# The low part of one weight load in four: a GpSimd-issued adding DMA in place of a VectorE subtraction

## The chip, the cores and the metric

One NeuronCore of a Trainium2 chip runs the whole program. The metric is the device time of one execution in microseconds (us).

In the text, TensorE (PE) multiplies matrices, VectorE (DVE) and ScalarE (ACT) work element by element, GpSimd (POOL) here only sets up constants, and SyncE (SP) issues the weight loads. A DMA transfer is issued by one of the engines' queues and carried out by 16 DMA engines that all queues share.

## The reference, cut to what matters

The reference is a two-layer encoder trunk on a sequence of 256 positions with 2048 features, in float32. Each layer normalises its input, multiplies it by a wide weight matrix, runs two token mixers (a bidirectional mLSTM and a bidirectional retention), and projects their outputs back:

```
h    = rmsnorm(x, norm_w)
proj = h @ w_in                                   # 2048 x 18448
q_m, k_m, v_m, z_m, o_m, g_m, q_r, k_r, v_r, z_r, gate_m, gate_r = split(proj)
...
y    = mix[:2048] * (u_m @ w_proj_m) + mix[2048:] * (u_r @ w_proj_r)
x    = x + y @ w_out                              # and a final rmsnorm
```

Nearly all of the work is in these products of a 256 x 2048 activation with 2048-row weights. What is computed of them does not change here, only how one operand is prepared.

## The kernel before

**Three multiplications for one.** TensorE is fed with a rounded format (`F32R`). So that the product stays accurate, each weight tile `raw` is split into a high part `whi` (the rounded weight) and a low part `wlo` (what the rounding lost), and so are the activations. `mm3` then adds three products into the same result: high by high, high activation by low weight, low activation by high weight.

**Blocks, loads and chunks.** The weights are worked off in blocks of 512 columns (the function `gemm`; eight of the 98 blocks, at the start of each layer, have 384 or 400 columns). The 2048 rows of a block come in four loads `i` = 0 to 3; each is one DMA from SyncE's queue into one of three `raw` buffers of 1 MB (128 partitions x 2048 elements). Each load makes two chunks (`half` = 0, 1; `KC` = 2, so 128 x 1024 elements each), so a block has the chunks 0 to 7, and the chunks 2 and 3 are those of load `i == 1`. A chunk is used by 12 matmuls (2 row groups of the weight, 2 halves of the sequence, 3 products).

**Who makes a chunk.** `wsplit` makes it: ScalarE writes `whi` as a rounded copy of `raw` (line 224), then VectorE writes `wlo` as `raw - whi` (line 225). There are three buffers of `whi` and three of `wlo`, so the parts of a chunk can be written when TensorE has done with the chunk three before it. A `raw` buffer can be loaded again when both of its chunks have been split. The last block of the program is done apart (tiles `wh` and `wl`).

**Order of the work.** Each engine has one queue that it works off in order. A scheduler sets the order; `tc.high_priority(offset=AHEAD)` lets the splitting and the loads of later chunks go ahead of the other work of ScalarE, VectorE and SyncE. Between chunks, `gemm` calls `run_later`, which puts in pieces of the attention work of earlier blocks, so that TensorE finds it between its blocks.

**Small row buffers.** The tag `row` holds 128 x 512 tiles: the mixing bias `bm`, the decay table `dec`, the last norm's weight `fw` and scratch of the first statistics `sq0`. `bm`, `dec` and `fw` are loaded from ScalarE's queue.

Of the kernel before, what the change touches and what calls it, by code (L numbers as in the profile page):

```python
# [9 lines left out]
F32 = mybir.dt.float32  # L10
F32R = mybir.dt.float32r
I32 = mybir.dt.int32
AF = mybir.ActivationFunctionType
ALU = mybir.AluOpType
AX = mybir.AxisListType

P = 128
# [5 lines left out]
NB = 512  # L23
# [6 lines left out]

# 512-column blocks of a layer's weights, in the order in which the host packs them
B_QK_M = 0
# [14 lines left out]
KC = 2  # L47
# [11 lines left out]
def encoder_kernel(ctx: ExitStack, tc: tile.TileContext, x, x_t, positions, w_main, w_qk0, w_qk1, b_mgate, vecs, b_mix,  # L59
                   final_norm_w, inv_freq, rpieces, decay, out):  # L60
    nc = tc.nc
# [3 lines left out]
    wp = ctx.enter_context(tc.tile_pool(name="wp", bufs=3))  # L65
    tmp = ctx.enter_context(tc.tile_pool(name="tmp", bufs=2))
# [7 lines left out]
    def t512(name, dtype=F32):  # L74
        return tmp.tile([P, 512], dtype, name=name, tag="t512", bufs=6)
# [3 lines left out]

# [1 line left out]
    x_sb = const.tile([P, NT, D], F32, name="x_sb")  # L81
# [36 lines left out]
    def late_setup():  # L118
# [28 lines left out]

        # adding and subtracting 1.5 * 2^(23 + b) rounds to a multiple of 2^b
        def drop_turns(v, magic):
# [22 lines left out]

# [1 line left out]
    def rsqrt_mean(dst, ss, n, count, base=EPS):  # L174
# [46 lines left out]

    def wsplit(raw, whi, wlo):
        with tc.high_priority(offset=AHEAD):
            nc.scalar.copy(out=whi, in_=raw)  # L224
            nc.vector.tensor_tensor(out=wlo, in0=raw, in1=whi.bitcast(F32), op=ALU.subtract)  # L225
# [24 lines left out]
    def gemm(xhi, xlo, src, name, n=NB, ahead=(), before=None):  # L250
        ps = [pg.tile([P, NB], F32, name=f"{name}{t}", tag="g")[:, 0:n] for t in range(NT)]
        for ck in range(NCK):
            if before is not None:
                before(ck)
            elif ck >= 3:
                run_later()
            i, half = divmod(ck, KD // KC)
            if half == 0:
                raw = ahead[i] if i < len(ahead) else wraw(src, i)
            whi = wp.tile([P, KC * NB], F32R, name="whi", tag="whi", bufs=3)[:, 0:KC * n]  # L260
            wlo = wp.tile([P, KC * NB], F32R, name="wlo", tag="wlo", bufs=3)[:, 0:KC * n]
            wsplit(raw[:, half * KC * n:(half + 1) * KC * n], whi, wlo)
            for k in range(KC):
                kt = ck * KC + k
                for t in range(NT):
                    mm3(ps[t], xhi, xlo, t, kt, whi[:, k * n:(k + 1) * n], wlo[:, k * n:(k + 1) * n],
                        kt == 0, kt == KT - 1)
        return ps
# [18 lines left out]
    def x_stat(c, ss, first=False):  # L287
        for t in range(NT):
            junk = tmp.tile([P, NB], F32, name="sq0", tag="row", bufs=4) if first else t512("sq")
            nc.scalar.activation(out=junk, in_=x_sb[:, t, c * NB:(c + 1) * NB], func=AF.Square,  # L290
                                 accum_out=ss[:, t * NBLK + c:t * NBLK + c + 1])
# [15 lines left out]
    def mlstm_gates(gates, gate_out):  # L307
        g4 = gates.rearrange("p t (d k h) -> p t d k h", d=2, k=2)

        # log-sigmoid, decays summed along the sequence in both directions  # L310
        def small(name):
# [30 lines left out]

        # stabilised gate weights
        wt = bigt("wt", 2)
# [141 lines left out]
    def ret_scores(h, qr_hi, qr_lo, st_out):  # L486
        dec = tmp.tile([P, NB], F32, name="dec", tag="row", bufs=4)
        nc.scalar.dma_start(out=dec[:, 0:3 * P], in_=decay[h])
# [31 lines left out]

# [1 line left out]
    ht_hi, ht_lo, ss_x = new_ht()  # L522
# [25 lines left out]
    for l in range(DEPTH):  # L548
        gate_out, hm_out = [], []

        # mLSTM queries and keys: convolution along the sequence, SiLU
        qk_hi, qk_lo = bigt("qkm_hi", 3, F32R), bigt("qkm_lo", 4, F32R)
# [37 lines left out]

        # mLSTM attention matrices, both directions joined
        at = bigt("at", 5, F32R)
# [12 lines left out]

        # retention: rotary queries and keys
        qr_hi, qr_lo = bigt("qkr_hi", 2, F32R), bigt("qkr_lo", 4, F32R)
# [33 lines left out]

        # mLSTM output gate and per-head statistics
        hm = hm_out[0]
# [16 lines left out]
        for b in range(NBLK):  # L660
            ps = gemm(ht_hi, ht_lo, wmain(l, B_Z_M + b), "zm")
            ev = []
            for t in range(NT):
                z = t512("z")
                nc.scalar.activation(out=z, in_=ps[t], func=AF.Silu, scale=rs[t])
                i = t * NH_M + b
# [7 lines left out]
        def branch(b_gate, u_hi, u_lo, b_proj, first):  # L674
            for b in range(NBLK):
                bm = tmp.tile([P, NB], F32, name="bm", tag="row", bufs=4)
                mc = (0 if first else D) + b * NB
# [40 lines left out]

        # output projection, residual
        if l < DEPTH - 1:  # L720
# [8 lines left out]

# [1 line left out]
    halves = NBLK + 1  # L731
# [22 lines left out]
    for b in range(NBLK):  # L754
        fw = tmp.tile([P, NB], F32, name="fw", tag="row", bufs=4)
        nc.scalar.dma_start(out=fw, in_=final_norm_w[b * NB:(b + 1) * NB].rearrange("(o n) -> o n", o=1)
# [41 lines left out]
def _pack(inputs):  # L798
    import numpy as np

    def chunks(w):
        # [2048, n] to [chunk, partition, (k n)]
        n = w.shape[1]
        return w.reshape(NLD, KD, P, n).transpose(0, 2, 1, 3).reshape(NLD, P, KD * n)
# [31 lines left out]
def _constants():  # L836
    import numpy as np
    freq = np.power(10000.0, -np.arange(64) / 64).astype(np.float32)[None, :]
    # 1 / (2 pi) in pieces of twelve significant bits
    digits = 0x28BE60DB9391054A7F09D5F47D4D3770  # L840
# [30 lines left out]
```

## Time and profile before

| what | value |
|---|---|
| time, median of 3 runs | 2237.16 us (2236.63 to 2237.55) |
| span of the profiled execution, first to last instruction | 2235.9 us |
| TensorE busy | 2218.1 us, 99% of the span |
| VectorE busy | 1331.9 us, 60% |
| ScalarE busy | 1086.0 us, 49% |
| GpSimd busy | 1.7 us, 0% |
| granted TensorE clock, mean | 0.999 of full speed |
| moved by DMA | 419.49 MB, 188 GB/s on average |

The profiled execution has no time of its own beside its span; the span is 1.3 us shorter than the median of the timed runs. Busy time counts the stretches in which an engine carries out at least one instruction. Matmuls overlap, so their single durations add up to more than the busy time of TensorE.

### The profile page before, as it was taken

How to read it: one execution, taken by the hardware profiler on the slowest of the kernel's cores; microseconds unless marked ns; L12 is line 12 of the kernel's file. 1: busy time of each engine (PE TensorE's matmuls, PEld its weight loads, DVE VectorE, ACT ScalarE, POOL GpSimd, SP SyncE). 2: the span in 40 equal slices, each digit the busy share in tenths (PEclk: the TensorE clock that was granted, in tenths of full speed). 3: DMA queues.
4: the chain of work that ended last, by engine and by line, in shares of the span. 5: the costliest groups of instructions: out<-in, count | busy, mean ns of one | idle time of the engine just before them, and what ended most of it. 6: DMA issues, size and time to landing. Idle time of an engine off the chain costs nothing.

```text
span 2235.9 us, 26069 instructions
## 1 busy us (share of the span) xinstructions
PE 2218.1 (99%) x10360; PEld 1868.6 (84%) x10360; DVE 1331.9 (60%) x1809; ACT 1086.0 (49%) x1380; POOL 1.7 (0%) x10
## 2 busy tenths in 40 slices
PE   8999999999999999999999999999999999999998
PEld 8888888888888888888898888888888888888887
DVE  6887665555555455555578746655555555555555
ACT  7654344555544454444457544445554434444444
POOL 0000000000000000000000000000000000000000
PEclk9999999999999999999999999999999999999999
DMA  7544455455555555555455445544555555555553
GB/s 281 189 156 167 175 190 186 177 190 188 189 196 197 203 187 189 196 190 195 171 169 195 153 166 188 195 167 182 198 186 191 203 193 196 186 195 191 199 190 148
DMA packets 66426, 419.49 MB, mean 188 GB/s; under 512 B 8192, under 2 KB 10496, under 8 KB 20224
## 3 DMA queue, kind: packets, MB, share of 16 engines
q1 hardware_dynamic: 61120, 409.44, 51.0%
q10 hardware_dynamic: 5184, 8.39, 1.1%
q8 instruction: 81, 1.33, 0.2%
q14 instruction: 41, 0.34, 0.0%
HBM read 415.70 MB, written 2.10 MB: 187 GB/s over the span
## 4 chain that ended last, share of the span: by engine, by line
PE 97%; DMA 1%; ACT 1%; DVE 0%; issue 0%; SPq 0%; ACTq 0%
PE gt L231 5%; PE gt L230 5%; PE pj L230 5%; PE gt L229 5%; PE pj L231 5%; PE pj L229 5%; PE vr L229 3%; PE wo L229 3%; PE wo L231 3%; PE vr L230 3%; PE vm L230 3%; PE vm L229 3%; PE wo L230 3%; PE zm L231 3%; PE om L229 3%; PE vr L231 3%
## 5 line engine op out<-in xcount | busy, mean ns | idle before, releaser
L225 DVE TENSOR_TENSOR wlo<-raw,whi 128x1024 fp32r<-128x1024 f32 (+2 forms) x776 | 933.0, 1203 | 818.0 <-ACT whi L224 816.6
L224 ACT CAST whi<-raw 128x1024 fp32r<-128x1024 f32 (+2 forms) x776 | 803.1, 1035 | 1007.1 <-PE gt L231 203.7
L229 PE MATMUL gt<-whi,ht_hi 128*128 128x512 f32 x512 | 200.1, 391 | 0.0
L231 PE MATMUL gt<-whi,ht_lo 128*128 128x512 f32 x512 | 199.3, 389 | 0.0
L230 PE MATMUL gt<-wlo,ht_hi 128*128 128x512 f32 x512 | 199.2, 389 | 0.0
L229 PE MATMUL qk<-whi,ht_hi 128*128 128x384 f32 (+2 forms) x320 | 112.3, 352 | 7.5 <-ACT whi L224 7.5
L230 PE MATMUL qk<-wlo,ht_hi 128*128 128x384 f32 (+2 forms) x320 | 112.5, 351 | 0.3 <-DVE wlo L225 0.3
L231 PEld LDWEIGHTS gt<-whi,ht_lo 128*128 128x128 f32 x512 | 96.1, 188 | 20.0
L230 PEld LDWEIGHTS gt<-wlo,ht_hi 128*128 128x128 f32 x512 | 96.2, 188 | 19.7
L229 PEld LDWEIGHTS gt<-whi,ht_hi 128*128 128x128 f32 x512 | 96.1, 188 | 19.7
L231 PE MATMUL qk<-whi,ht_lo 128*128 128x384 f32 (+2 forms) x320 | 111.9, 350 | 0.0
L229 PE MATMUL zm<-whi,ht_hi 128*128 128x512 f32 x256 | 100.2, 391 | 0.0
L229 PE MATMUL qr<-whi,ht_hi 128*128 128x512 f32 x256 | 100.2, 391 | 0.0
L229 PE MATMUL zr<-whi,ht_hi 128*128 128x512 f32 x256 | 100.2, 391 | 0.0
L229 PE MATMUL vr<-whi,ht_hi 128*128 128x512 f32 x256 | 100.1, 391 | 0.0
L230 PE MATMUL vr<-wlo,ht_hi 128*128 128x512 f32 x256 | 99.9, 390 | 0.0
L229 PE MATMUL vm<-whi,ht_hi 128*128 128x512 f32 x256 | 99.9, 390 | 0.0
L230 PE MATMUL vm<-wlo,ht_hi 128*128 128x512 f32 x256 | 99.7, 390 | 0.0
L231 PE MATMUL vm<-whi,ht_lo 128*128 128x512 f32 x256 | 99.7, 389 | 0.0
L231 PE MATMUL zm<-whi,ht_lo 128*128 128x512 f32 x256 | 99.7, 389 | 0.0
L231 PE MATMUL qr<-whi,ht_lo 128*128 128x512 f32 x256 | 99.7, 389 | 0.0
L231 PE MATMUL zr<-whi,ht_lo 128*128 128x512 f32 x256 | 99.7, 389 | 0.0
(255 smaller groups left out, 4205.7 us busy)
## 6 DMA issues: line engine op xcount, KB each, us to landing
raw<-in_w_main_dram SPq DMA_DIRECT2D x360, 1024.0 KB, 4.8
raw<-in_w_qk_dram SPq DMA_DIRECT2D x24, 768.0 KB, 4.5
bm<-in_b_mix_dram ACTq DMA_DIRECT2D x16, 256.0 KB, 4.2
raw<-in_w_qk_dram SPq DMA_DIRECT2D x5, 800.0 KB, 4.3
dec<-in_decay_dram ACTq DMA_DIRECT2D x16, 192.0 KB, 3.5
raw<-in_w_qk_dram SPq DMA_DIRECT2D x6, 400.0 KB, 7.0
x_sb<-in_x_dram SPq DMA_DIRECT2D x4, 512.0 KB, 8.9
out_dram<-pre SPq DMA_DIRECT2D x8, 256.0 KB, 3.0
```

The lines of the kernel that those rows point to most:

```text
L224: nc.scalar.copy(out=whi, in_=raw)
L225: nc.vector.tensor_tensor(out=wlo, in0=raw, in1=whi.bitcast(F32), op=ALU.subtract)
L229: nc.tensor.matmul(out=ps, lhsT=xhi[:, o:o + P], rhs=whi, start=first, stop=False)
L230: nc.tensor.matmul(out=ps, lhsT=xhi[:, o:o + P], rhs=wlo, start=False, stop=False)
L231: nc.tensor.matmul(out=ps, lhsT=xlo[:, o:o + P], rhs=whi, start=False, stop=last)
```

## The change

For the chunks of load `i == 1` (every block but the last), `wsplit` gets `queue=True`. ScalarE first writes `wlo` as the negated weight, rounded to `F32R`; then a DMA issued by GpSimd adds `raw` onto it inside the transfer (`accum_op=ALU.add`), so that `wlo` becomes `raw` minus the rounded weight; then ScalarE makes `whi` as before. VectorE does nothing for these chunks. `wlo` gets a fourth buffer, and the tag `row` goes from four buffers to two. The rest of the diff removes comments.

```
-    def wsplit(raw, whi, wlo):
+    def wsplit(raw, whi, wlo, queue=False):
         with tc.high_priority(offset=AHEAD):
+            if queue:
+                nc.scalar.activation(out=wlo, in_=raw, func=AF.Copy, scale=-1.0)
+                nc.gpsimd.dma_start(out=wlo, in_=raw, accum_op=ALU.add)
+                nc.scalar.copy(out=whi, in_=raw)
+                return
             nc.scalar.copy(out=whi, in_=raw)
             nc.vector.tensor_tensor(out=wlo, in0=raw, in1=whi.bitcast(F32), op=ALU.subtract)
...
-            wlo = wp.tile([P, KC * NB], F32R, name="wlo", tag="wlo", bufs=3)[:, 0:KC * n]
-            wsplit(raw[:, half * KC * n:(half + 1) * KC * n], whi, wlo)
+            wlo = wp.tile([P, KC * NB], F32R, name="wlo", tag="wlo", bufs=4)[:, 0:KC * n]
+            wsplit(raw[:, half * KC * n:(half + 1) * KC * n], whi, wlo, i == 1)
...
-            junk = tmp.tile([P, NB], F32, name="sq0", tag="row", bufs=4) if first else t512("sq")
+            junk = tmp.tile([P, NB], F32, name="sq0", tag="row", bufs=2) if first else t512("sq")
...
-        dec = tmp.tile([P, NB], F32, name="dec", tag="row", bufs=4)
+        dec = tmp.tile([P, NB], F32, name="dec", tag="row", bufs=2)
...
-                bm = tmp.tile([P, NB], F32, name="bm", tag="row", bufs=4)
+                bm = tmp.tile([P, NB], F32, name="bm", tag="row", bufs=2)
...
-        fw = tmp.tile([P, NB], F32, name="fw", tag="row", bufs=4)
+        fw = tmp.tile([P, NB], F32, name="fw", tag="row", bufs=2)
```

What stands in the queues shows the change in three places. Lines of the changed kernel are five higher (line 225 of it is the negation, 227 the `whi` copy behind it, 229 the ordinary `whi` copy).

The first place is ScalarE's queue where a block named `pj` (a projection) follows a block named `gt` (a gate) in the first layer, at about 651 us of the trace of before. The first two rows are chunks 0 and 1 of the `pj` block, and the rows `mix` finish the block before it. Before:

```order
L224 CAST whi_5252<-raw_5250 128x1024
L224 CAST whi_5268<-raw_5250 128x1024
L224 CAST whi_5286<-raw_5284 128x1024
L684 ACTIVATE mix_5242<-mix_5242 128x512
L684 ACTIVATE mix_5245<-mix_5245 128x512
L678 DMA bm_6908<-in_b_mix_dram 128x512
L224 CAST whi_5302<-raw_5284 128x1024
L224 CAST whi_5320<-raw_5318 128x1024
L224 CAST whi_5336<-raw_5318 128x1024
```

In the changed kernel, the two negations of chunks 2 and 3 stand directly behind the `whi` copy of chunk 1, ahead of the `whi` copies of the same two chunks:

```order
L229 CAST whi_5308<-raw_5306 128x1024
L229 CAST whi_5324<-raw_5306 128x1024
L225 ACTIVATE wlo_5343<-raw_5340 128x1024
L225 ACTIVATE wlo_5360<-raw_5340 128x1024
L227 CAST whi_5342<-raw_5340 128x1024
L689 ACTIVATE mix_5298<-mix_5298 128x512
L689 ACTIVATE mix_5301<-mix_5301 128x512
L227 CAST whi_5359<-raw_5340 128x1024
L683 DMA bm_5736<-in_b_mix_dram 128x512
L229 CAST whi_5378<-raw_5376 128x1024
```

The negation of chunk 2 moves up to the copy of chunk 1, that of chunk 3 comes before the copy `whi` of chunk 2; the `bm` that is loaded here is the one two blocks of its kind ahead, where before it was four ahead.

The second place is TensorE's queue, chunk 2 of the first `pj` block, with the semaphores that it waits for. Before, the first matmul on `wlo` waits for VectorE:

```order
L229 MATMUL pj_4962<-whi,um_hi 128x512 [waits Activation_49]
L230 MATMUL pj_4962<-wlo,um_hi 128x512 [waits DVE_49]
L231 MATMUL pj_4962<-whi,um_lo 128x512
L229 MATMUL pj_4963<-whi,um_hi 128x512
L230 MATMUL pj_4963<-wlo,um_hi 128x512
L231 MATMUL pj_4963<-whi,um_lo 128x512
```

In the changed kernel the same matmul, the second of the chunk, waits for the GpSimd-issued DMA (`DMASW`):

```order
L234 MATMUL pj_5014<-whi,um_hi 128x512 [waits Activation_49]
L235 MATMUL pj_5014<-wlo,um_hi 128x512 [waits DMASW4_49]
L236 MATMUL pj_5014<-whi,um_lo 128x512
L234 MATMUL pj_5015<-whi,um_hi 128x512
L235 MATMUL pj_5015<-wlo,um_hi 128x512
L236 MATMUL pj_5015<-whi,um_lo 128x512
```

The order of the matmuls is the same; the wait on `wlo` has moved from VectorE to a transfer. Behind it on TensorE's queue stands all later work.

The third place is the start of the program on ScalarE, where the first block of 400 columns is split while the activations `ht_hi` are made. Before:

```order
L275 ACTIVATE ht_hi<-xt,vec_sb 128x256
L224 CAST whi<-raw 128x800 x2
L275 ACTIVATE ht_hi<-xt,vec_sb 128x256 x7
L224 CAST whi<-raw 128x800 x2
L275 ACTIVATE ht_hi<-xt,vec_sb 128x256 x4
L224 CAST whi<-raw 128x800 x2
L275 ACTIVATE ht_hi<-xt,vec_sb 128x256 x4
```

The changed kernel has the negations of chunks 2 and 3 there:

```order
L280 ACTIVATE ht_hi<-xt,vec_sb 128x256
L229 CAST whi<-raw 128x800 x2
L280 ACTIVATE ht_hi<-xt,vec_sb 128x256 x7
L225 ACTIVATE wlo<-raw 128x800
L227 CAST whi<-raw 128x800
L225 ACTIVATE wlo<-raw 128x800
L227 CAST whi<-raw 128x800
L280 ACTIVATE ht_hi<-xt,vec_sb 128x256 x2
L229 CAST whi<-raw 128x800
L280 ACTIVATE ht_hi<-xt,vec_sb 128x256 x2
L229 CAST whi<-raw 128x800
```

The copies `whi` of chunks 2 and 3 stand one instruction and two instructions later, and each negation stands directly ahead of its copy. GpSimd's queue holds 194 such transfers, two for each of 97 blocks (178 of 128 x 1024 elements, 12 of 128 x 768, 4 of 128 x 800), and nothing else behind the constants. On SyncE's queue the load that takes over a buffer of `i == 1` waits for the two transfers instead of VectorE.

## Rows read from the trace of the kernel before

**Rows 1.** The page, its head and part 1.

```profile
span 2235.9 us, 26069 instructions
...
PE 2218.1 (99%) x10360; PEld 1868.6 (84%) x10360; DVE 1331.9 (60%) x1809; ACT 1086.0 (49%) x1380; POOL 1.7 (0%) x10
```

**Rows 2.** Waits of TensorE, all: who waited for whom, us, times, longest.

```profile
PE qk L229 <- ACT whi L224: 7.5, 1, 7.5
PE tr L397 <- ACT qk_sb L580: 1.3, 1, 1.3
PE qk L230 <- DVE wlo L225: 0.3, 1, 0.3
PE pc L333 <- DVE lf L328: 0.2, 1, 0.2
```

**Rows 3.** Windows: busy us of each engine (instructions), clock, DMA share, GB/s.

```profile
80.00:100.00 20.00, 18.69 (x89) 15.86 (x88) 15.25 (x25) 18.48 (x35) 0.00 (x0) 1.00 0.51 197
100.00:2200.00 2100.00, 2099.62 (x9707) 1758.28 (x9707) 1241.73 (x1612) 1004.07 (x1240) 0.00 (x0) 1.00 0.52 186
2000.00:2236.00 236.00, 227.97 (x1067) 190.87 (x1066) 129.87 (x147) 100.65 (x119) 0.00 (x0) 0.99 0.50 182
```

**Rows 4.** Timeline of ScalarE at 651 us: start, length, line, instruction, idle before.

```profile
651.46 1.05 ACT L224 CAST whi<-raw 128x1024 fp32r<-128x1024 f32 x1 [1.67 <-PE gt L231]
654.18 1.06 ACT L224 CAST whi<-raw 128x1024 fp32r<-128x1024 f32 x1 [1.67 <-PE gt L231]
```

**Rows 5.** Timeline of TensorE at 654 us, the first two instructions of a block.

```profile
653.98 0.39 PE L229 MATMUL pj<-whi,um_hi 128*128 128x512 f32 x1
654.20 0.39 PE L230 MATMUL pj<-wlo,um_hi 128*128 128x512 f32 x1
```

**Rows 6.** Timeline of VectorE at 652 us.

```profile
652.54 1.23 DVE L225 TENSOR_TENSOR wlo<-raw,whi 128x1024 fp32r<-128x1024 f32 x1 [1.50 <-ACT whi L224]
653.69 1.40 DVE L683 SCALAR_TENSOR_TENSOR mix<-gt,rstd,bm 128x512 f32<-128x512 f32 x2
...
658.03 1.22 DVE L225 TENSOR_TENSOR wlo<-raw,whi 128x1024 fp32r<-128x1024 f32 x1 [1.54 <-ACT whi L224]
```

**Rows 7.** Groups of instructions by line and shape: count, busy us, mean ns.

```profile
L225 DVE TENSOR_TENSOR wlo<-raw,whi 128x1024 fp32r<-128x1024 f32 x712 | 871.7, 1224 | 791.6 <-ACT whi L224 790.9
L225 DVE TENSOR_TENSOR wlo<-raw,whi 128x768 fp32r<-128x768 f32 x48 | 45.7, 956 | 16.3 <-ACT whi L224 15.7
...
L684 ACT ACTIVATE mix<-mix 128x512 f32<-128x512 f32 x32 | 18.8, 624 | 0.0
```

**Rows 8.** Waits of the DMA queue of SyncE.

```profile
SPq L219 <- DVE wlo L225: 1841.8, 357, 8.8
```

**Rows 9.** The page, parts 3 and 6: queue; issues with KB each, us to landing.

```profile
q1 hardware_dynamic: 61120, 409.44, 51.0%
...
raw<-in_w_main_dram SPq DMA_DIRECT2D x360, 1024.0 KB, 4.8
...
bm<-in_b_mix_dram ACTq DMA_DIRECT2D x16, 256.0 KB, 4.2
...
raw<-in_w_qk_dram SPq DMA_DIRECT2D x6, 400.0 KB, 7.0
x_sb<-in_x_dram SPq DMA_DIRECT2D x4, 512.0 KB, 8.9
```

**Rows 10.** Timeline of the start: ScalarE, then TensorE.

```profile
10.98 0.84 ACT L224 CAST whi<-raw 128x800 fp32r<-128x800 f32 x1
...
14.16 0.35 PE L230 MATMUL qk<-wlo,ht_hi 128*128 128x400 f32 x1
...
23.54 0.45 PE L230 MATMUL qk<-wlo,ht_hi 128*128 128x400 f32 x1 [0.34 <-DVE wlo L225]
```

**Rows 11.** Timeline of ScalarE, a 384-column block.

```profile
29.92 0.84 ACT L224 CAST whi<-raw 128x768 fp32r<-128x768 f32 x1 [1.05 <-PE qk L231]
32.00 0.84 ACT L224 CAST whi<-raw 128x768 fp32r<-128x768 f32 x1 [1.24 <-PE qk L231]
```

## The prediction

> **What bounds the kernel now.** The page's head comes first: TensorE is busy for 2218.1 of 2235.9 us [rows 1], so 17.8 us are all that it ever stands idle. The list of its waits says where: one wait of 7.5 us for the first weights, and after it nothing above 1.3 us; for `wlo` it waited once, 0.3 us [rows 2]. The windows place the rest: between 100 and 2200 us it idles 0.4 us of 2100, and 8.0 us lie in the last 236 [rows 3]. In the bulk the time is thus the number of matmuls times their spacing. VectorE is busy for 59% of that window and ScalarE for 48%, and nobody waits for either. VectorE's share of the split is not what the time is made of; what counts is whether a chunk's `wlo` still arrives before TensorE reads it.
>
> **How much room a chunk has.** Two `whi` copies in a row start at 651.46 and 654.18 [rows 4]: one chunk takes TensorE 2.72 us, and each copy waits until TensorE is done with the chunk three before. The `pj` block starts at 653.98 and its first matmul on `wlo` at 654.20 [rows 5], so the copy at 651.46 is that of its chunk 1, and chunk 2 has its `wlo` read at 653.98 + 2 x 2.72 + 0.22 = 659.64. By the order, the negation of chunk 2 stands right behind the copy of chunk 1: from 652.51, and, at the 1.05 us of a copy of the same shape, to 653.56. (Two 512-column activations of 624 ns would make it 1.25 [rows 7], 0.2 us worse; I take the copy, whose shape is the same.) The first transfer has 659.64 - 653.56 = 6.1 us from there, 6.0 with its start. The negation of chunk 3 has its buffer free, thanks to the fourth one, when the chunk before the block ends: 654.18 to 655.23, against a read at 662.36, so 7.1 us. In a 384-column block the copies are 2.08 us apart and last 0.84 [rows 11]: three chunks less 0.64 us each, and two ScalarE instructions 0.21 us shorter each, leave 6.0 - 1.9 + 0.4 = 4.5 us.
>
> **What the transfer takes.** The trace shows no GpSimd-issued and no adding transfer, so I build it from the loads. The load queue kept the 16 DMA engines busy for 51.0% of 2235.9 us with 409.44 MB, 2.92 us for 1024 KB; these landed 4.8 us after issue [rows 9], so 1.9 us are lag.
> - Moving 512 KB: 1.46 us if only the written bytes count, 2.92 if `raw` and `wlo` are both read through the same engines. Nothing is nearer to either; I take the middle, 2.2.
> - Standing beside a load: `raw` loads go out when VectorE ends the second `wlo` of a load [rows 8], which for chunk 1 is 652.54 + 1.23 = 653.77 [rows 6], within 0.2 us of the first transfer. So they share the engines every time. From 0 to the load's whole 2.92; the 256 KB `bm` transfer, issued beside loads, landed after 4.2 us, of which 1.9 + 0.73 are its own and 1.6 waiting. For more bytes I take 1.9.
> - GpSimd making the descriptors: 0 to 1.22 (one VectorE subtraction in front of it, if it has to wait for one [rows 7]); I take 0.5.
>
> Together 1.9 + 2.2 + 1.9 + 0.5 = 6.5 us, between 3.4 (1.9 + 1.46) and 8.9 (1.9 + 2.92 + 2.92 + 1.2). The upper end is what a 512 KB `x_sb` load took in the crowded start, 8.9 [rows 9].
>
> The Trainium skill, page "DMA: Bandwidth & Descriptors", section "Anatomy of one DMA — SWDGE (gpsimd) path", fits a GpSimd-issued transfer as 2.0 us plus its bytes at 436 GB/s. For 512 KB that is an estimate of 3.2 us, with which the sum of this prediction would be that of the first rival. The same fit gives 4.4 us for a 1024 KB load, where the trace has 4.8; no run so far shows an adding transfer.
>
> **The change part by part.**
> - Taken from VectorE: 178 subtractions of 1.224 us, 12 of 0.956 and 4 of about 1, some 233 us [rows 7]. All of it lies under TensorE; worth 0.
> - Added to ScalarE: as many negations of 1.05 and 0.84 us, about 201 us. In the bulk they fit into the 1.67 us that ScalarE idles ahead of each copy [rows 4]: 0. Between 80 and 100 us it is already busy for 18.48 of 20 us while TensorE idles 1.3 [rows 3]; two negations there cost up to 2 us. I take 2.
> - First transfer of a full block: 6.5 against 6.05, late by 0.45 us. Each block begins anew, because the negation hangs on TensorE's own progress, so nothing is paid ahead: 89 blocks (712 subtractions, eight a block [rows 7]) x 0.45 = 40 us. TensorE's queue is in order, so all of its work waits.
> - Second transfer: issued at 655.3 but moved behind the first, which lands at 660.1; 2.2 us later is 662.3, before 662.36. Its read is pushed back by the first stall as well: 0.
> - The six 384-column blocks: three quarters of the moving and sharing, 1.9 + 3.1 + 0.5 = 5.5 against 4.5, late by 1.0: 6 us.
> - The two 400-column blocks: in the first, `raw` for chunk 2 is copied at 10.98, so the negation ends at 11.8; a 400 KB load in that crowded stretch took 7.0 us [rows 9], which makes 18.8, and `wlo` was read at 14.16 [rows 10]. That is 4.6 late, less the 0.34 that TensorE waits at 23.54 anyway: 4. The second, in layer two, 1.
> - `raw` is freed later: the second transfer lands at 662.3, where VectorE was done at 658.03 + 1.22 = 659.25 [rows 6]. The next block's first copy needs that load at 653.98 + 6 x 2.72 + 0.2 = 670.5, and 662.3 + 4.8 is 667.1, some 2 us more when it shares: hidden, with 1.4 us left. Then the `whi` copy would be late next.
> - Two `row` buffers in place of four: `bm` and `dec` are still loaded a block or more ahead of their use, against a landing of 4.2: 0.
>
> The sum is 40 + 6 + 4 + 1 + 2 = 53 us. The execution's span of 2235.9 us becomes 2289; what lies around it is 1.3 us, the difference to the median of 2237.2, so 2290 us.
>
> **The rivals.**
> 1. *Hidden in the bulk.* The transfer lands in under 6.0 us in full blocks, because the bytes are moved once and the load gives way. For it: bounds down to 3.4. Against it: the load is issued at the same moment. Only the start, the 384-column blocks and ScalarE's busy stretch then pay: 4 to 13 us, 2241 to 2250 us, and at its lower end it is no measurable change. It decides at 6.0 us from issue to landing.
> 2. *Adding is slow.* Reading two operands, sharing with the load and waiting for the descriptors all come at their upper bounds: 8.9 us, 2.85 late in 89 blocks = 254, with 16 for the 384-column blocks and 10 at the start: about 2515 us. From 8 us on `raw` is also late and `whi` waits. For it: the `x_sb` row; against it: that stretch is more crowded than the bulk. The forecast ends, and this begins, at about 7.6 us (2385 us).
> 3. *Relief pays.* With 194 subtractions gone, VectorE finishes evacuations sooner. It could win only what TensorE idles: 17.8 us less the first 7.5 and most of the last 8.0, some 2 us, 2235 us, and only if every transfer is hidden, also at the start. That ends on the other side of the forecast.
>
> **How the numbers follow.** About 0.2% (4.5 us) is what a measurement of this kernel tells from no change. Late by 0.1 to 1.6 us (2250 to 2385): 0.43. Rival 1: 0.32, of which 0.14 stays within 4.5 us. Rival 2: 0.20. Rival 3: 0.05, of which 0.03 is faster by more than that. So faster 0.03, same 0.16, slower 0.81. The forecast is the likeliest case's 2290 (its own range 2250 to 2385); the range to hold it 8 times in 10 reaches into both rivals, 2239 to 2440, leaving out some 0.08 below and 0.12 above.
>
> **What would show it.** In the profile after, TensorE's list of waits should have a row for `wlo` released by a DMA, some 90 times at around half a microsecond, at the second matmul of chunk 2 and not of chunk 3; the transfers should land about 6.5 us after issue; VectorE's busy time should fall by about 233 us and ScalarE's rise by about 201. A wait at chunk 3 would say that moving costs more than 2.7 us a transfer. No such row in the bulk would make rival 1 right, waits of 2 us or more rival 2, a wait of `whi` for `raw` would say that the load has become late. A stall at the start of well under 4 us would break the term of the first block.

## The result and the profile after

The changed kernel takes 2699.82 us (median of 4 runs, 2690.26 to 2701.14), the kernel before 2237.36 us beside it (2236.63 to 2238.07): a ratio of 1.2057, 95% interval [1.2043, 1.2072]. It is 462 us slower, where 53 were forecast and 203 were the end of the range. One of the four runs of experiment 5 was slow (2806.70 us, at a granted clock of 0.85); the ratio given there leaves it out, and without it the median is 2582.12 us.

The head and part 1 of the page after, against [rows 1]:

```profile
span 2699.3 us, 26899 instructions
PE 2385.6 (88%) x10360; PEld 1968.3 (73%) x10360; DVE 1109.0 (41%) x1615; ACT 1258.1 (47%) x1574; POOL 168.0 (6%) x204
```

The span grew by 463.4 us. VectorE is busy for 223 us less and ScalarE for 172 us more, where 233 and 201 were forecast. The moved instructions themselves add up to 232.8 and 201.6 us in the pages; the busy times differ by less because instructions that follow each other directly overlap, as in [rows 6], where one ends at 653.77 and the next starts at 653.69. TensorE has the same 10360 matmuls, but is busy for 167.5 us longer with them, and it now idles 313.7 us instead of 17.8. These are two losses and not one, and a reader who looks only for waits misses the first.

The waits of TensorE after, against [rows 2] (who waited for whom, us, times, longest):

```profile
PE pj L235 <- DMA wlo<-raw: 52.2, 16, 3.5
PE gt L235 <- DMA wlo<-raw: 49.5, 16, 4.3
PE qk L235 <- DMA wlo<-raw: 38.0, 10, 8.3
...
PE qk L234 <- ACT whi L229: 7.2, 1, 7.2
```

All rows with `wlo<-raw` together are 297.7 us in 95 waits: about one for each of the 97 blocks, 3.1 us each. Here is one of them, in the `pj` block that follows a `gt` block; ScalarE's negation for chunk 2, the issue of a load by SyncE, the issue of the transfer by GpSimd, then TensorE's first matmul on its `wlo`, against [rows 4] and [rows 5]:

```profile
725.81 1.06 ACT L225 ACTIVATE wlo<-raw 128x1024 fp32r<-128x1024 f32 x1
727.20 0.33 SPq L219 DMA_DIRECT2D raw<-in_w_main_dram  x1
727.27 0.87 POOL L226 DMA_DIRECT2D wlo<-raw  x1 [25.05 <-DVE wlo L230]
...
732.82 0.39 PE L234 MATMUL pj<-whi,um_hi 128*128 128x512 f32 x1
736.55 0.50 PE L235 MATMUL pj<-wlo,um_hi 128*128 128x512 f32 x1 [3.34 <-DMA wlo<-raw]
...
738.81 0.63 PE L235 MATMUL pj<-wlo,um_hi 128*128 128x512 f32 x1
739.24 0.63 PE L236 MATMUL pj<-whi,um_lo 128*128 128x512 f32 x1
...
740.52 0.40 PE L236 MATMUL pj<-whi,um_lo 128*128 128x512 f32 x1
```

The list counts the wait from the end of the matmul before, at 732.82 + 0.39 = 733.21. Matmuls start 0.23 us apart, so without the wait this one would have started at 733.05, which is 5.8 us behind the issue at 727.27: the room of 6.0 us was read nearly right. But the transfer takes 9.2. Then look at the spacing of the starts: 0.43 us behind the stall, where they were 0.23 us in the kernel before and ahead of the stall. The windows around this stall (busy us and instructions of PE, PEld, DVE, ACT, POOL; granted clock; DMA share; GB/s) say why:

```profile
725.00:732.00 7.00, 7.00 (x33) 5.79 (x32) 2.55 (x3) 6.49 (x7) 1.73 (x2) 1.00 0.59 185
732.00:736.50 4.50, 1.21 (x6) 0.67 (x4) 1.23 (x1) 1.81 (x3) 0.00 (x0) 1.00 1.04 229
736.50:740.50 4.00, 3.95 (x10) 3.11 (x11) 0.00 (x0) 0.00 (x0) 0.00 (x0) 0.58 0.57 115
740.50:745.00 4.50, 4.50 (x21) 3.70 (x20) 1.38 (x2) 2.10 (x2) 0.00 (x0) 1.00 0.85 255
```

In the 4.0 us behind the stall the granted clock is 0.58, so TensorE is at its lower level of 1.2 GHz for most of them, and then at 2.4 GHz again. Nine spacings take 740.52 - 736.55 = 3.97 us instead of 9 x 0.227 = 2.04: 1.9 us more, on top of the 3.3 (3.5 by the spacing) that the stall itself costs. The mean granted clock fell from 0.999 to 0.941, and 0.058 x 2699.3 us is 157 us: most of the 167.5 us by which TensorE's busy time grew.

Parts 3 and 6 of the page, against [rows 9]:

```profile
q1 hardware_dynamic: 61120, 409.44, 46.1%
q0 software_dynamic: 27936, 99.69, 18.7%
...
raw<-in_w_main_dram SPq DMA_DIRECT2D x360, 1024.0 KB, 4.8
wlo<-raw POOLq DMA_DIRECT2D x178, 512.0 KB, 9.3
...
bm<-in_b_mix_dram ACTq DMA_DIRECT2D x16, 256.0 KB, 8.0
```

The transfers land 9.3 us after issue. That is the median of first and second ones; read one by one from the trace, the first ones of a block have a median of 8.9 us and the second ones of 9.8. The median load lands as before, after 4.8 us, but one load in four stands beside the transfers, and those take 6.5 us (median) where every fourth load took 4.8 before. Per megabyte, GpSimd's queue q0 kept the 16 engines for 18.7% x 2699.3 / 99.69 = 5.1 us, the load queue q1 for 3.0.

Who is served first is to be read from the same block on the DMA queues. The load went out at 727.20 us and the transfer at 727.27. The lines give the landings of the two, then the packets (each transfer has 27936 / 194 = 144 of them, the 128 rows of its tile and 16 small ones; a load likewise) that each queue started between 727.27 and 732.00, and then between 732.00 and 733.50:

```profile
raw<-in_w_main_dram SPq DMA_DIRECT2D x1, 1024.0 KB, 6.5
wlo<-raw POOLq DMA_DIRECT2D x1, 512.0 KB, 9.2
...
q1 hardware_dynamic: 112, 0.92, 68.1%
...
q0 software_dynamic: 49, 0.20, 66.9%
q1 hardware_dynamic: 32, 0.13, 35.1%
```

In the first 4.7 us, 112 of the load's 128 rows start and none of the transfer's. The transfer does not share the engines with the load: it stands behind it.

### The profile page after: what moved, and what is told of

Read it like the earlier page. It is cut to its first block, busy times and chain, and to the rows that moved or that the text cites. A ratio compares the mean times of both kernels' runs of the same rounds, so it can differ in the third digit from the quotient of the medians.

```text
span 2699.3 us, 26899 instructions
## 1 busy us (share of the span) xinstructions
PE 2385.6 (88%) x10360; PEld 1968.3 (73%) x10360; DVE 1109.0 (41%) x1615; ACT 1258.1 (47%) x1574; POOL 168.0 (6%) x204
## 3 DMA queue, kind: packets, MB, share of 16 engines
q0 software_dynamic: 27936, 99.69, 18.7%
## 4 chain that ended last, share of the span: by engine, by line
PE 58%; DMA 31%; issue 9%; ACT 0%; POOLq 0%; DVE 0%; SPq 0%; ACTq 0%
DMA wlo<-raw 31%; PE pj L235 3%; PE gt L235 3%; PE pj L236 3%; PE pj L234 3%; PE gt L236 3%; PE gt L234 3%; PE vm L235 2%; PE wo L235 2%; PE qk L235 2%; PE vr L235 2%; PE zm L235 2%; PE om L235 2%; PE qr L235 2%; PE zr L235 2%
## 5 line engine op out<-in xcount | busy, mean ns | idle before, releaser
L230 DVE TENSOR_TENSOR wlo<-raw,whi 128x1024 fp32r<-128x1024 f32 (+2 forms) x582 | 700.2, 1203 | 1377.7 <-ACT whi L229 1377.0
L226 POOL DMA_DIRECT2D wlo<-raw x194 | 166.4, 858 | 2475.3 <-DVE wlo L230 1951.6
L235 PE MATMUL gt<-wlo,ht_hi 128*128 128x512 f32 x512 | 210.1, 410 | 49.5 <-DMA wlo<-raw 49.5
L225 ACT ACTIVATE wlo<-raw 128x1024 fp32r<-128x1024 f32 (+2 forms) x194 | 201.6, 1040 | 23.3 <-PE gt L235 7.7
L235 PE MATMUL pj<-wlo,ur_hi 128*128 128x512 f32 x256 | 106.5, 416 | 26.0 <-DMA wlo<-raw 26.0
L235 PE MATMUL pj<-wlo,um_hi 128*128 128x512 f32 x256 | 105.1, 410 | 26.2 <-DMA wlo<-raw 26.2
L235 PE MATMUL zm<-wlo,ht_hi 128*128 128x512 f32 x256 | 105.2, 411 | 25.6 <-DMA wlo<-raw 25.6
L235 PE MATMUL om<-wlo,ht_hi 128*128 128x512 f32 x256 | 104.9, 410 | 24.7 <-DMA wlo<-raw 24.7
L235 PE MATMUL zr<-wlo,ht_hi 128*128 128x512 f32 x256 | 104.7, 409 | 24.4 <-DMA wlo<-raw 24.4
L235 PE MATMUL qr<-wlo,ht_hi 128*128 128x512 f32 x256 | 104.7, 409 | 23.9 <-DMA wlo<-raw 23.9
```

Of the source, the lines that this page charges most:

```text
L225: nc.scalar.activation(out=wlo, in_=raw, func=AF.Copy, scale=-1.0)
L226: nc.gpsimd.dma_start(out=wlo, in_=raw, accum_op=ALU.add)
L235: nc.tensor.matmul(out=ps, lhsT=xhi[:, o:o + P], rhs=wlo, start=False, stop=False)
```

## The experiments

**1. VectorE adds.** Everything of the change stays (ScalarE's negation, its place in the queue, four `wlo` and two `row` buffers); only the addition is VectorE's again.

```
-                nc.gpsimd.dma_start(out=wlo, in_=raw, accum_op=ALU.add)
+                nc.vector.tensor_tensor(out=wlo, in0=raw, in1=wlo.bitcast(F32), op=ALU.add)
```

> Everything of the change but the transfer: ScalarE negates, VectorE (not a DMA) adds raw onto wlo; four wlo buffers, two row buffers. Theory (the time is the late transfer and what its stall does to the clock): no wait of TensorE for wlo above 0.3 us, granted clock 0.99 or more, 2235 to 2245 us. Rival (ScalarE's 201 us of negations and the moved instructions cost part of the 463 us): well above 2245, 2300 or more, with waits for ScalarE in the list.

Measured: 2237.43 us against 2237.51, ratio 1.000 [0.9991, 1.001]. Part 1 of its page, and one window:

```profile
PE 2218.0 (99%) x10360; PEld 1868.5 (84%) x10360; DVE 1321.1 (59%) x1809; ACT 1259.9 (56%) x1574; POOL 1.7 (0%) x10
80.00:100.00 20.00, 19.60 (x92) 16.51 (x90) 13.62 (x20) 19.94 (x36) 0.00 (x0) 1.00 0.47 168
```

ScalarE carries 174 us more and costs nothing, also between 80 and 100 us, where it is busy for 19.94 of 20 us. That is what was expected. So the whole loss hangs on the transfer.

**2. No load beside the transfer.** The load of `i == 1` is left out and chunks 2 and 3 are made from the buffer of load 0, so the values are others. With one load less in four, no load is issued while a first transfer is under way.

```
-            if half == 0:
+            if half == 0 and i != 1:
                 raw = ahead[i] if i < len(ahead) else wraw(src, i)
```

> The load i == 1 is left out and its chunks are made from the load before (a quarter of the weights is not used, each block has 3 loads), so that no load is issued in the 2.7 us around the first adding transfer. Theory (the transfer stands behind the load on the DMA engines for about 3.4 of its 9.3 us): first landing about 6 us after issue, waits for wlo mostly gone or below 0.5 us, 2240 to 2290 us. Rival (the long time from issue to the first moved byte belongs to the GpSimd-issued queue itself): landing stays above 9 us, waits of about 3.1 us a block, 2650 to 2700 us.

Measured: 2249.89 us, ratio 1.0051 [1.0035, 1.0067]. The transfer's row, the only sizable wait for it, and the rows that its queue started in the 2.5 us behind an issue at 658.66:

```profile
wlo<-raw POOLq DMA_DIRECT2D x178, 512.0 KB, 5.0
PE qk L235 <- DMA wlo<-raw: 2.8, 4, 1.6
...
q0 software_dynamic: 61, 0.25, 51.6%
```

The same adding transfer lands after 5.0 us when it is alone (the first ones after 4.5), fits its room, and the loss is nearly gone; 12.4 of 462 us are left. Its first row starts 1.4 us behind the issue (median), where it started after 4.9 us beside the load. Of the 9.3 us, 4.3 come from the load beside it.

**3. High parts first.** Chunks 2 and 3 are worked off together, first all 16 matmuls on `whi`, then the 8 on `wlo`, which gives the transfers some 3 us more. The order of summation changes, nothing else.

```
+            if i == 1:
+                held.append((ck, whi, wlo))
+                if half == 0:
+                    continue
+                for lo in (False, True):
+                    for c, wh, wl in held:
...
+                                for a, b in ([(xhi, wl)] if lo else [(xhi, wh), (xlo, wh)]):
+                                    nc.tensor.matmul(out=ps[t], lhsT=a[:, o:o + P], rhs=b[:, ks], start=False,
+                                                     stop=False)
```

> The matmuls of chunks 2 and 3 are put in another order: the 16 that need whi first, then the 8 that need wlo; the transfers are unchanged. The first read of wlo moves back by 15 x 0.227 = 3.4 us, to 9.4 us after the negation, against a landing of 9.3. Theory (lateness alone, the clock following the stall): waits of 0 to 0.5 us a block, clock 0.98 or more, 2240 to 2300 us with landing unchanged at about 9.3. Rival (the transfers slow matmuls in other ways, through memory traffic): TensorE stays busy for some 2380 us and the time stays above 2400 without long waits.

Measured: 2359.87 us, ratio 1.0547 [1.0531, 1.0563]. The transfers land no earlier (9.4 us), but the waits for them fall to 81.4 us in 83 and the granted clock is back at 0.992. So lateness of that one operand is what costs. The time is 60 us above the expected range all the same. Of the waits, 69 us in 71 are for chunk 3's transfer, which lands later than chunk 2's and is now read four matmuls, 0.9 us, behind it; and TensorE is busy for 43 us longer than before.

**4. A copy from GpSimd's queue.** The transfer copies `raw` over `wlo` instead of adding, so that `wlo` is the weight itself.

```
-                nc.gpsimd.dma_start(out=wlo, in_=raw, accum_op=ALU.add)
+                nc.gpsimd.dma_start(out=wlo, in_=raw)
```

> The GpSimd-issued transfer copies raw over wlo in place of adding onto it (so the low part is wrong; bytes written, issue and order are the same). Theory (an adding transfer reads two operands, 2.6 us for 8 rows of 4 KB on each engine): half of the moving time goes, landing about 8.0 us, waits of about 1.9 us a block, 2500 to 2570 us. Rival (adding costs nothing of its own): landing 9.3 and 2690 us as before.

Measured: 2471.99 us, ratio 1.1048 [1.1025, 1.1072]; TensorE waits 173.4 us in 93 waits. Its queue and its transfer:

```profile
q0 software_dynamic: 27936, 99.69, 10.9%
wlo<-raw POOLq DMA_DIRECT2D x178, 512.0 KB, 7.5
```

Adding costs 1.8 of the 9.3 us (1.3 of the 8.9 of the first ones). Per megabyte the queue keeps the engines for 10.9% x 2474.8 / 99.69 = 2.7 us instead of 5.1. The copy brings back 228 of the 462 us, 28 us more than the expected range allowed. But it is still too late, and a load beside it costs more than the adding does.

**5. Work in the place of the stall.** 14 matmuls into a spare PSUM tile stand between chunk 2's first matmul on `whi` and its first on `wlo`.

```
         nc.tensor.matmul(out=ps, lhsT=xhi[:, o:o + P], rhs=whi, start=first, stop=False)
+        if fill:
+            spare = aux("spare")
+            for _ in range(fill):
+                nc.tensor.matmul(out=spare[:, 0:whi.shape[-1]], lhsT=xhi[:, o:o + P], rhs=whi, start=True, stop=True)
```

> In each of the 97 blocks 14 extra matmuls on high parts, into a spare PSUM tile that nobody reads, stand between chunk 2's first matmul on whi and its first on wlo, so that TensorE works through the 3.1 us in which it stood idle in the changed kernel. They add 14 x 0.227 = 3.2 us of work a block, about 305 us in all. Theory (the clock is lost because TensorE stood idle): the waits for wlo fall under 40 us in all, the granted clock stays at 0.98 or more, and the time is that of the kernel before plus the filler, 2237 + 305 = about 2545 us (2535 to 2580), some 150 us FASTER than the changed kernel although it does more. Rival (the clock falls for another reason, such as the transfers themselves or the power of all engines together): the granted clock stays near 0.94 and the time at 2690 us or more.

Measured: 2582.99 us, ratio 1.1539 [1.1516, 1.1562], granted clock 0.996. Part 1 of its page, and its longest wait for `wlo`:

```profile
PE 2542.9 (98%) x11718; PEld 2119.9 (82%) x11718; DVE 1110.2 (43%) x1615; ACT 1260.0 (49%) x1574; POOL 168.1 (7%) x204
PE qk L239 <- DMA wlo<-raw: 10.2, 7, 6.3
```

With 1358 matmuls more, the kernel is 117 us faster than the changed one. The transfers land as late as before (9.4 us) and move the same bytes; only TensorE no longer stands idle for them. So the clock fell because of the stall and not because of the transfers. The time came out 38 us above the expected centre, 3 us outside its range: 19.6 us of waits are left, and TensorE's busy time grew by 324.8 us, of which the filler explains some 302; the other 23 us are not explained.

**6. Half the transfer.** GpSimd's transfer makes only the first half of the chunk's columns (256 KB in rows of 2048 bytes), VectorE the other.

```
+                m = raw.shape[-1] // 2
+                nc.scalar.activation(out=wlo[:, 0:m], in_=raw[:, 0:m], func=AF.Copy, scale=-1.0)
+                nc.gpsimd.dma_start(out=wlo[:, 0:m], in_=raw[:, 0:m], accum_op=ALU.add)
                 nc.scalar.copy(out=whi, in_=raw)
+                nc.vector.tensor_tensor(out=wlo[:, m:], in0=raw[:, m:], in1=whi[:, m:].bitcast(F32), op=ALU.subtract)
```

> Only the first half of the chunk's columns goes through the transfer (256 KB in 128 rows of 2048 bytes instead of 512 KB in rows of 4096); VectorE makes the other half from the rounded weight as in the kernel before. Theory (a landing is a delay behind the load, about 4.3 us, plus about 1.4 us of start, plus a moving time in proportion to the bytes, about 3.6 us for 512 KB): 9.3 - 1.8 = 7.5 us, waits of 1.3 us a block where they were 3.1, some 125 us in all, and a clock loss of 30 to 100 us: 2390 to 2470 us. Rival (the price is set by the 128 rows and not by their bytes): the landing stays above 8.8 us and the time above 2620 us.

Measured: 2412.61 us, ratio 1.0787 [1.0771, 1.0803]; landing 7.5 us, waits 139.5 us, clock 0.994. Half the bytes save 1.8 us (1.3 for the first ones), about as much as was expected of a time in proportion to the bytes.

**7. Half the load beside it.** The load of `i == 3`, which runs beside the transfers, brings only half its columns, and both of its chunks are made from that half (other values, same work).

```
+        if pieces == 1 and i == 3:
+            n //= 2
```

> The fourth load of each block, the one that runs beside the transfers, brings only half its columns (512 KB instead of 1024 KB, in rows of half the length), and both of its chunks are made from that half; the work on chip stays the same, the values differ. Theory (the transfer stands behind whatever of the load is still to come): the 4.3 us that the load adds become about 2.1, the landing of the 512 KB transfers falls from 9.3 to 7.2 us, the waits from 3.1 to about 1.0 us a block, some 100 us in all; with the clock's loss 2340 to 2430 us. Rival (a load beside it costs a fixed price, a switch between queues): the landing stays above 8.7 us and the time above 2600 us.

Measured: 2393.49 us, ratio 1.0696 [1.068, 1.0712]; waits 111.8 us. The transfer, and the halved load:

```profile
wlo<-raw POOLq DMA_DIRECT2D x178, 512.0 KB, 7.0
raw<-in_w_main_dram SPq DMA_DIRECT2D x90, 512.0 KB, 4.5
```

9.3, 7.0 and 5.0 us with a whole load, half a load and none beside it (8.9, 6.9 and 4.5 for the first ones): the price goes with the load's bytes, as it must if the transfer stands behind them.

**8. The copy from a hardware queue.** The copy of experiment 4, issued by ScalarE instead of GpSimd.

```
-                nc.gpsimd.dma_start(out=wlo, in_=raw, accum_op=ALU.add)
+                nc.scalar.dma_start(out=wlo.bitcast(F32), in_=raw)
```

> The transfer is a plain copy of raw over wlo, without adding (so that what it leaves in wlo is the weight itself), and it is issued from ScalarE's hardware queue instead of GpSimd's; to be compared with the same copy from GpSimd's queue (landing 7.5 us, 2472 us). Theory (a GpSimd-issued transfer is served last beside a load on a hardware queue, a hardware queue gets its share at once): the landing falls to 4.5 to 5.8 us, less than the 6.5 us of room, the waits for wlo fall under 20 us in all and the time is 2237 to 2260 us. Rival (anything issued behind a 1024 KB load waits for it, whichever queue it is on): the landing stays at 7 us or more and the time at 2430 us or more.

Measured: 2266.73 us, ratio 1.013 [1.0115, 1.0145]; 17.7 us of waits, 14.6 of them in five `qk` blocks. The copies land after 4.8 us, where GpSimd's took 7.5. Landing and waits are as expected, the time is 7 us above its range. The expectation puts the gain down to the queue. But the order differs as well. ScalarE issues the copy 0.03 us behind its own negation, GpSimd 0.40 us behind it (727.27 against 725.81 + 1.06 in the block above), so in 83 of the 89 full blocks ScalarE's copy goes out some 0.3 us ahead of the load, where GpSimd's went out 0.07 us behind it. In the other six the load is 0.1 to 0.4 us ahead. One block of either kind, each with the landing of its copy:

```profile
649.90 0.48 ACTq L226 DMA_DIRECT2D wlo<-raw  x1
650.20 0.33 SPq L219 DMA_DIRECT2D raw<-in_w_main_dram  x1
wlo<-raw ACTq DMA_DIRECT2D x1, 512.0 KB, 5.2
...
1214.14 0.33 SPq L219 DMA_DIRECT2D raw<-in_w_main_dram  x1
1214.25 0.47 ACTq L226 DMA_DIRECT2D wlo<-raw  x1
wlo<-raw ACTq DMA_DIRECT2D x1, 512.0 KB, 7.7
```

The six copies behind their load land after 6.9 to 9.2 us (median 7.3), as late as GpSimd's, the others after a median of 5.0. The other way round, experiment 4 has one full block in which GpSimd's copy goes out 0.72 us ahead of the load, and that one lands after 3.2 us:

```profile
214.09 0.53 POOL L226 DMA_DIRECT2D wlo<-raw  x1 [25.64 <-ACT wlo L225]
214.81 0.33 SPq L219 DMA_DIRECT2D raw<-in_w_main_dram  x1
wlo<-raw POOLq DMA_DIRECT2D x1, 512.0 KB, 3.2
```

So it is the order and not the kind of queue that delays the transfer. The load pays in turn: the one beside the copies lands after 6.0 us (median) in this run, 4.8 in the kernel before.

**9. The load behind the transfers.** Nothing is left out. GpSimd copies one column of chunk 3's `whi` into the buffer of load 3 before it, so that this load goes out behind both transfers (except in the very first block, whose loads are taken ahead).

```
+            if ck == 3 and not ahead:
+                got[2] = wraw(src, 2)
+                with tc.high_priority(offset=AHEAD):
+                    got[3] = wraw_(src, 3, 1, whi)
...
+        if behind is not None:
+            nc.gpsimd.tensor_copy(out=raw[:, 0:1], in_=behind[:, 0:1].bitcast(F32))
```

> The changed kernel with nothing left out; only the order on the queues differs. The fourth load of a block, which ran beside the transfers, is held back: GpSimd copies one column of chunk 3's rounded weight into the load's buffer before it, so that the load can only start when both transfers have been issued (one GpSimd instruction more a block). Theory (a GpSimd-issued transfer waits for the bytes of a load ahead of it on a hardware queue): the first transfer has no load beside it, the landing falls from 9.3 us to 5.0 to 6.0 us, under the 6.5 us of room, the waits for wlo fall under 25 us in all, and the granted clock is back at 0.99 or more: 2237 to 2262 us, as fast as the kernel before within 1% and some 440 us faster than the changed kernel, but not faster than the kernel before. Rival (what delays the transfer is not this load but its own start or the other queues): the landing stays above 8 us and the time above 2550 us. A second way to fail: the load comes too late for chunk 6, which would show as TensorE waits on whi or as ScalarE waits on raw.

Measured: 2282.16 us, ratio 1.0201 [1.0186, 1.0216]. The transfer's row, its largest wait, and two windows:

```profile
wlo<-raw POOLq DMA_DIRECT2D x178, 512.0 KB, 5.5
PE qk L237 <- DMA wlo<-raw: 20.5, 8, 9.4
0.00:100.00 100.00, 78.07 (x410) 74.88 (x411) 52.64 (x135) 58.49 (x95) 9.25 (x21) 0.93 0.75 236
100.00:2200.00 2100.00, 2081.72 (x9577) 1733.41 (x9576) 1015.13 (x1425) 1160.21 (x1426) 172.48 (x273) 1.00 0.73 229
```

The first transfers land after 4.5 us, as without a load. An order on the queues brings back 418 of the 462 us, and in the bulk the clock is 1.00 again. It is 20 us above the expected end of 2262 all the same: 9.4 us is one wait in the very first block, whose load 3 was not held back, and TensorE is busy for 17.9 us less between 100 and 2200 us than before [rows 3]. Behind 100 us its list has 10.5 us of waits for the transfers and 6.7 us for `whi` and VectorE's `wlo`: the second way to fail that was named, but small.

**10. The load in quarters.** Load 3 goes out as four loads of a quarter of the columns, in rows of 2048 bytes instead of 8192.

```
+        if i == 3 and pieces == 1:
+            pieces = 4
```

> The fourth load of each block is issued as four loads of a quarter of the columns (256 KB each, rows of 2048 bytes instead of 8192); bytes and values stay the same. Theory (the transfer's first bytes wait until the load's bytes ahead of them are through, whatever their pieces): landing 8.8 to 9.5 us and 2620 to 2720 us. Rival (queues take turns by rows, and the long rows of the load crowd out the transfer's): with rows of a quarter of the length the transfer's share grows, the landing falls to 8 us or less and the time under 2520 us.

Measured: 2530.04 us, ratio 1.1298 [1.1272, 1.1324]; landing 8.4 us, waits 198.0 us, clock 0.972. It falls between the two. SyncE issues the four pieces one after another, the last 1.3 us behind the first; in the block at 717 us they land after 3.5, 5.1, 8.5 and 9.9 us, the transfer, issued 0.07 us behind the first piece, after 7.7. So it overtakes a part of the load. Shorter rows and later pieces came together here, and the run does not tell them apart.

**11. The load on GpSimd's queue.** Load 3 is issued by GpSimd.

```
-            nc.sync.dma_start(out=raw[:, ps], in_=part[:, ps])
+            (nc.gpsimd if pieces == 1 and i == 3 else nc.sync).dma_start(out=raw[:, ps], in_=part[:, ps])
```

> The fourth load of each block is issued by GpSimd, on the queue of the transfers and mostly ahead of both of them in its program, instead of by SyncE on a hardware queue. Theory (the transfer stands behind the bytes of a load issued ahead of it; on one queue it stands behind them in order): landing of the first transfer 8 us or more and a time above 2500 us. Rival (only a hardware queue goes ahead of GpSimd's, and without one beside it the transfer starts as early as without any load): landing 5 to 6.5 us and 2240 to 2300 us.

Measured: 2317.96 us, ratio 1.0362 [1.0344, 1.0379]; landing 6.6 us (4.6 for the first ones), waits 55.1 us. Landing and time are a little above the rival's, but the expectation rested on an order that the run had in few blocks only. GpSimd's timeline, one block of the usual kind and one of the other, with the landing of the first transfer of the latter:

```profile
643.25 0.85 POOL L226 DMA_DIRECT2D wlo<-raw  x1 [19.58 <-DVE wlo L230]
645.47 0.76 POOL L219 DMA_DIRECT2D raw<-in_w_main_dram  x1
...
1251.94 0.56 POOL L219 DMA_DIRECT2D raw<-in_w_main_dram  x1 [21.51 <-DVE wlo L230]
1252.56 0.85 POOL L226 DMA_DIRECT2D wlo<-raw  x1
wlo<-raw POOLq DMA_DIRECT2D x1, 512.0 KB, 8.8
```

As a rule the load stands behind both transfers, not ahead of them, and the run is a second form of experiment 9 and agrees with it. In four full blocks the load is 0.6 us ahead of the first transfer, and there this lands after 8.3 to 8.9 us: a load on the same queue is not gone around either.

## Why the prediction was wrong, by its own steps

The kernels side by side (landing of the 512 KB transfers, 256 KB in number 6, as the page has it; median landing of the first transfers of all blocks; all waits of TensorE for them; its busy time; all us):

| kernel | landing | first ones | waits | TensorE busy | clock | time |
|---|---|---|---|---|---|---|
| before | - | - | - | 2218.1 | 0.999 | 2237.4 |
| after | 9.3 | 8.9 | 297.7 | 2385.6 | 0.941 | 2699.8 |
| 10, load in quarters | 8.4 | 7.7 | 198.0 | 2315.8 | 0.972 | 2530.0 |
| 4, copy | 7.5 | 7.6 | 173.4 | 2285.3 | 0.981 | 2472.0 |
| 6, half transfer | 7.5 | 7.6 | 139.5 | 2254.1 | 0.994 | 2412.6 |
| 7, half load | 7.0 | 6.9 | 111.8 | 2261.6 | 0.994 | 2393.5 |
| 3, high parts first | 9.4 | 8.9 | 81.4 | 2261.1 | 0.992 | 2359.9 |
| 11, load on GpSimd's queue | 6.6 | 4.6 | 55.1 | 2244.9 | 0.992 | 2318.0 |
| 9, load behind | 5.5 | 4.5 | 24.6 | 2235.6 | 0.995 | 2282.2 |
| 8, copy from ScalarE's queue | 4.8 | 5.0 | 17.7 | 2231.0 | 0.996 | 2266.7 |
| 2, no load beside | 5.0 | 4.5 | 3.1 | 2222.6 | 0.999 | 2249.9 |

- **Room, place and direction: right.** The room of 6.0 us was 5.8 in the block shown. The wait stands at chunk 2's second matmul in 95 of 97 blocks and not at chunk 3, whose transfer has the first stall to hide in. TensorE waits for `whi` once, 7.2 us at the start, so `raw` is never late, although the second rival had it late from 8 us on. ScalarE's share is hidden (experiment 1 measured 0 for it, with 2 us forecast), and no run shows a gain from the relief of VectorE.
- **"Standing beside a load": the step that failed.** The prediction had the transfer share the engines with the load, bounded the price by the load's own 2.92 us of engine time and took 1.9; experiment 2 measures 4.3. They do not share alike: where the load's rows come to the engines first, the transfer stands behind nearly all of them (112 of 128 in the block above).
- **What decides who stands behind.** A load's first row starts 0.95 us behind its issue and that of GpSimd's transfer 1.4 us, where nothing is in the way (medians, before and experiment 2). So the load, issued 0.07 us ahead, comes first by half a microsecond, and the transfer's first row starts only after 4.9 us. With the load held back (experiment 9) the transfer lands early; in the few blocks of experiments 4, 8 and 11 where the order is turned, so is the lateness, on ScalarE's queue as on GpSimd's. To be issued first is not enough: in experiment 6 GpSimd's transfer goes out 0.36 us ahead of the load in most blocks, still has the later first row, and lands no earlier than in the blocks where it goes out behind. The `bm` row from which 1.9 was scaled could not show this: in the bulk of the kernel before (at 655.13, for one) `bm` is issued 1.3 us behind its load, when part of the load is through.
- **Moving and starting: right.** 1.9 + 2.2 + 0.5 = 4.6 us were forecast without a load; first transfers take 4.5, the median of all is 5.0. By the queue's 5.1 us per megabyte 0.524 MB take 2.7 us, inside the bounds of 1.46 to 2.92 and near the upper one. The estimate of 3.2 us that stands beside the prediction's sum is met only by the copy of experiment 4 that came ahead of its load.
- **The sum of the upper bounds**, 8.9 us, is what the first transfers took, and the second rival's stall of 2.85 us is near the mean of 3.1. That is luck in part: adding is the smaller share (1.3 us), the load cost 4.4 where its bound was 2.92, and start and moving came to 4.5 where their bounds add up to 6.0. With the stall about right, its 2515 us are still 185 short, since it had no term for the clock.
- **A term that was missing: the clock.** The prediction priced a stall at its own length. In the windows above TensorE comes back at 0.58 of its clock, and of the 463.4 us, 167.5 are longer busy time, some 157 of them the clock. Experiment 5 shows that the idling causes its fall. The Trainium skill, page "TensorE: Matmul & The Clock Gate", section "HAM oscillation — how this bites in real kernels", tells of matmuls behind a long DMA wait that run at half rate, each time anew; the trace agrees, with 0.58, and the rule speaks against this change. In the table the busy time grows faster than the waits: by 36 us for 139.5 us of waits, and by 167.5 for 297.7. By that trend the term would have been small against the forecast stalls of 0.45 us; against 3 us it is half as much again. Not all of the growth is the clock: in experiment 6 the clock of 0.994 makes 0.005 x 2409.6 = 12 of the 36 us. A part of the rest is that the matmul ahead of a wait counts its whole 0.39 us as busy and not the 0.23 to the next one; what else there is stays open.
- **The first block**: forecast 4 us, measured one wait of 8.3 us there, since the transfer, issued at 11.80, let TensorE go on at 23.50, after 11.7 us in place of 7.0.

**What stays open.** Why a transfer that comes behind a load stands behind nearly all of it is not settled. The Trainium skill, page "DMA: Bandwidth & Descriptors", section "Queues, rings and completion order", says that each DMA engine takes turns between the queues packet by packet, and that it finishes a whole packet, typically 9 to 17 descriptors, before it switches. If a row is one descriptor, a load has 8 of them on each of the 16 engines (an estimate from its 128 rows), which can be one packet in that sense; 112 rows of the load ahead of the transfer's first agree with that. How large a packet is on these queues, no run here shows, and experiment 10, which changed the rows, changed the order with them. That the order decides is shown by changing it (experiment 9) and by the blocks that have it otherwise; no run put the adding transfer from GpSimd's queue ahead of the load by an earlier issue alone.

## What to carry to other kernels

Before an operand that TensorE reads soon is moved to a DMA transfer, look at what else is issued around its issue, to tenths of a microsecond, and at how long each queue takes to its first row: behind a 1 MB load the transfer landed after 9.3 us here, alone after 5.0, and holding the load back behind it (experiment 9) brought back 418 of 462 us. Price a repeated stall of TensorE at its length plus the slower matmuls behind it, and read both, the waits and the engine's busy time, since the second loss shows in no list of waits. And where nobody waits for the engine that is relieved, as for VectorE here (0.5 us in all, [rows 2]), relief has nothing to win.

## What the runs showed that was not expected

- A 512 KB copy within the chip that comes ahead of a 1 MB load lands after 3.2 us from GpSimd's queue (one block) and 5.0 us from ScalarE's; one that comes behind it lands after 7.6 and 7.3 (medians). The load beside it lands after 6.4 us (experiment 4) and 6.0 (experiment 8) instead of 4.8.
- An adding transfer keeps the DMA engines for 5.1 us per megabyte, a copying one on the same queue for 2.7.
- The 256 KB `bm` loads from ScalarE's queue, at 4.2 us before, land after 8.0 us, issued behind the adding transfers; without the load ahead of these (experiment 2), after 5.3.
- A stall of 3.3 us was followed by 4.0 us with a granted clock of 0.58.
